# A hybrid decoder layer on one core: the first feed-forward product in a new order, its activation sums on another engine

## The chip, the core and the metric

The kernel runs on one core of a Trainium2 chip. A core has five engines, each with its own queue of instructions that it works off in order: TensorE (PE in the profile; matmuls into PSUM, with PEld for its weight loads), VectorE (DVE), ScalarE (ACT), GpSimd (POOL) and SyncE (SP), which here issues the DMAs. They meet through semaphores. SBUF holds the working tiles, PSUM eight banks of 128 x 512 float32 into which matmuls accumulate. The metric is the time of one execution on the device in microseconds.

## The reference

One decoder layer over 2048 tokens of width 1024, in float32:

```python
h = x + mixed @ w_out                       # mixed: gated linear attention and dilated window attention
nm = rmsnorm(h, mlp_norm_g)
a = jnp.square(jax.nn.relu(nm @ w_ff1))     # 2048 x 1024 times 1024 x 4096
h = h + a @ w_ff2                           # 2048 x 4096 times 4096 x 1024
y = rmsnorm(h, final_norm_g)
```

The change lies in the third line, and in loads for the fourth.

## The kernel before

The stages follow one another: input projection, attention, output projection, first feed-forward product, second feed-forward product. Each float32 operand of a matmul is split into a rounded high part (ScalarE, line 485) and the rest (VectorE, line 486, `split`), and three matmuls (lines 141 to 143, `mm3`) stand for one.

**First product.** The tokens are cut in two halves; the 4096 columns of w_ff1 in 16 groups of 256 (`NP`). A group of one half is a 2 x 2 block product in Strassen's manner, with seven products instead of eight: `jobs1` lists 2 x 16 groups of seven, 224 in all. Each product has four chunks of depth and so 12 matmuls of 128 x 128 by 128 x 512. For one half, the seven combinations of token blocks are kept in SBUF (`TB`, tiles hb), split; `norm_to_T` has written them to DRAM (`hTD`), and `reload` brings one back and splits it in two pieces of 1024 columns. During the last group of the first half, and a little beyond it, the seven of the second half are reloaded product by product (`parts_at`, lines 1570 to 1583).

`prep1(at + 2)` runs ahead of `product1(at)`. It splits the combination of w_ff1 for a product into one of four buffers (`combs1`), and makes the next combinations in place in the raw weights (w1raw, two buffers of 1 MB) with four adds of 512 columns on VectorE. Once the last product of a group has been split, `load_w1(g + 2)` loads the weights of the group after the next into the buffer that has come free. The scheduler may move an instruction ahead of others on its queue by times that it has planned. So the first add of a group (line 1300), which needs only its weights, stands in VectorE's queue almost a group ahead.

`product1` takes one of eight PSUM banks in rotation (`bank`, tags a, c, d, o) for each product. Its results are combined in SBUF: with P1 to P7 the products and X a scratch tile, in the order 1, 2, 5, 6, 3, 4, 7: X = P1; c11 = P2 + X; c22 = P5; X = P6 + X; c12 = X + c22; c12 = P3 + c12; c21 = P4; X = P7 + X; c21 = c21 + X; c22 = c22 + X. Copies run on ScalarE, the seven adds on VectorE. ScalarE then makes relu and square of each of the four blocks, in place. An even group writes them to one of two tiles (`even`), an odd group to one tile (`odd`).

**Sums for the second product.** The second product is a block product of its own with 26 products (`PRODUCTS`), whose left factors are sums of blocks of the activations. After each pair of groups `act_sums` makes them: 28 additions (`SUMS`) of 128 x 256, five after the even group (`EARLY`) and 23 after the odd one, all on GpSimd (line 1333). 22 of them are factors; they go through a ring of eight slots, and each pair is stored to DRAM (`actD`) by SyncE (line 1335). Four more factors are blocks as they are (`single`, line 1362). In all 16 x 28 = 448 additions.

**Second product.** 26 passes of four steps of 24 matmuls. A step's right factor is a combination of w_ff2 (`update_b`: a load, and additions on GpSimd or VectorE, line 1490), split by `prep_b`; its left factor is loaded from `actD` (`load_a`) and split by `prep_a`. The first two steps are prepared within the last products of the first stage (lines 1584 to 1595). At a pass's second step `begin` allocates the outputs whose first use is that pass and loads h into them (line 1536, two loads of 512 KB for each of eight tiles: one tile in pass 0, two in each of passes 1 to 3, one in pass 4). `taken` adds a pass's banks to its outputs during the next pass (line 1543).

SyncE's queue holds all these loads and stores. One that waits, for a sum or a buffer, holds up those behind it. `tc.keep_in_program_order` keeps a DMA from being moved ahead of what the program has before it.

Of the kernel before, what the change touches and what calls it, by code (L numbers as in the profile page):

```python
# [13 lines left out]
AF = mybir.ActivationFunctionType  # L14
# [55 lines left out]
EARLY = 5  # L70
# [45 lines left out]
def emit(tc, a, stop=99):  # L116
# [248 lines left out]
    def bank():  # L365
        banks[0] += 1
        return ps("acao"[banks[0] % 4])
# [906 lines left out]

    w1 = a["w_ff1"].rearrange("o (c p) n -> p (o c) n", p=128)
    NP = FF // 256
    jobs1 = [(g, j) for g in range(2 * NP) for j in order]
    raw1, combs1, acc1 = [], [], []

# [7 lines left out]
    def prep1(at):  # L1287

        if at >= len(jobs1):
            return  # L1290
        g, j = jobs1[at]
        if not combs1:
            combs1.extend(view(c[:, 1024 * q:], (2, 4, 128)) for c in [slot("w1comb", FR) for _ in range(2)]
                          for q in range(2))
        r = raw1[g % 2]
        (a11, a12), (a21, a22) = [[r[:, 4 * k:4 * k + 4, n * 128:n * 128 + 128] for k in range(2)] for n in range(2)]
        c = combs1[at % 4]
        split(c[:, 0], c[:, 1], {1: a11, 2: a12, 5: a21, 6: a21, 3: a12, 4: a22, 7: a21}[j])
        if j == 2:
            V.tensor_tensor(a21, a21, a22, op=OP.add)  # L1300
        if j == 5:
            V.tensor_tensor(a21, a21, a11, op=OP.subtract)  # L1302
            V.tensor_tensor(a12, a12, a21, op=OP.subtract)
        if j == 6:
            V.tensor_tensor(a21, a22, a21, op=OP.subtract)
        if j == 7:
            load_w1(g + 2)

    tags = list("acdcadco")
# [2 lines left out]
        tags.append(tags.pop(0))  # L1312
        return ps(tags[-1])

    xs1, ring1, even, odd = [], [], [], []

    def act_block(name, cs):

# [4 lines left out]
    def act_sums(half, q, cs, which):  # L1323

        if not ring1:
            ring1.extend([view(slot("ring1"), (8, 256)), view(xs1[0][:, 1024:], (4, 256))])
        outs_, temps = ring1
        for name, _, x, op, y in which:
            at = MADE.index(int(name)) if name[0] != "t" else None
            value = lambda v: (act_block(v, cs) if v[0] == "a" else temps[:, int(v[1])] if v[0] == "t"  # L1330
                               else outs_[:, MADE.index(int(v)) % 8])
            dst = temps[:, int(name[1])] if at is None else outs_[:, at % 8]
            G.tensor_tensor(dst, value(x), value(y), op=OP.add if op == "+" else OP.subtract)  # L1333
            if at is not None and at % 2:
                SP.dma_start(actD[at - 1:at + 1, :, q, half].rearrange("r p s -> p r s"), outs_[:, at % 8 - 1:at % 8 + 1])

    def product1(at):
        g, j = jobs1[at]
# [8 lines left out]
        X = xs1[0][:, 512 * par:512 * par + 512]  # L1347
        c11, c12, c21, c22 = [C4[:, n] for n in range(4)]
        both = (even[q % len(even)], C4)
        p = bank()  # L1350
        B, W = TB[j], combs1[at % 4]
        for c in range(4):
            mm3(p, W[:, 0, c], W[:, 1, c], B[0][:, c], B[1][:, c], c == 0, c == 3)

        def square(v):
            A.activation(v, v, AF.Relu)  # L1356
# [4 lines left out]
                if int(name[2]) % 2 == par and 2 * (int(name[2]) // 2) + int(name[1]) // 2 == n:  # L1361
                    SP.dma_start(actD[AT[r], :, q, half], act_block(name, both))

        if j in (1, 5, 4):
            A.activation({1: X, 5: c22, 4: c21}[j], p, AF.Copy)  # L1365
        elif j == 2:
            V.tensor_tensor(c11, p, X, op=OP.add)
            square(c11)
            single(0)
        elif j == 6:  # L1370
            V.tensor_tensor(X, p, X, op=OP.add)
            V.tensor_tensor(c12, X, c22, op=OP.add)
        elif j == 3:
            V.tensor_tensor(c12, p, c12, op=OP.add)  # L1374
            square(c12)
            single(1)
        else:
            V.tensor_tensor(X, p, X, op=OP.add)
            V.tensor_tensor(c21, c21, X, op=OP.add)
            V.tensor_tensor(c22, c22, X, op=OP.add)  # L1380
            square(c21)
            single(2)
            square(c22)
            single(3)
            act_sums(half, q, both, SUMS[EARLY:] if par else SUMS[:EARLY])

    tiles = [8 * half + i + 4 * k for half in range(2) for i in range(4) for k in range(2)]
    nxt = mix_T(tiles[0])
# [137 lines left out]
    def begin(ph):  # L1526

        if "g" not in fin and ph >= 2:
            v = slot("gf")
            fin["g"], fin["scr"] = v[:, :D], v[:, D:2 * D]  # L1530
            SP.dma_start(fin["g"], bcast_row(a["final_norm_g"], D))
        for (k, m), n in began.items():
            if n == ph:
                acc2[k, m] = view(slot("sum"), (4, 512))
                for h in range(2):
                    SP.dma_start(acc2[k, m][:, 2 * h:2 * h + 2],
                                 h6[k // 2, k % 2, :, h, :, 512 * m:512 * m + 512])

    def taken(ph, i, p):

# [33 lines left out]
    for at in range(7, len(jobs1)):  # L1574
        if at == first - 2:
            halves.update({n: reload(order[n], 1) for n in range(2)})
        prep1(at + 2)
        product1(at)
        for n in parts_at.get(at, ()):
            next(halves[n])  # L1580
# [98 lines left out]
```

## Time and profile before

| | |
|---|---|
| median of 3 runs | 2327.23 us (2323.65 to 2327.23) |
| the profiled execution | 2321.99 us, span 2320.2 us |
| mean granted TensorE clock | 0.993 |
| first feed-forward product, first to last matmul start | 1073.0 to 1718 us of the span |
| VectorE idle until the weights landed, before line 1300 | 97.7 us, 30 times |
| SyncE waiting at line 1335 for GpSimd's sums, 1080 to 1700 us | 383.7 us, 159 times |
| TensorE waiting for the low parts of w_ff1, 1080 to 1700 us | 17.2 us, 16 times |

A row of a timeline gives the start in us from the span's start, the duration, the engine, the line, the operation with output and inputs, and in square brackets the idle time of the engine before it and what ended it. A row of busy time by stretch gives the busy us and the number of instructions of each engine, the granted clock, and the share and rate of the DMA engines. An instruction's duration on VectorE overlaps the next one's by some 0.08 us, so queues are counted by the distance of starts.

### The profile page before, as it was taken

How to read it: one execution, taken by the hardware profiler on the slowest of the kernel's cores; microseconds unless marked ns; L12 is line 12 of the kernel's file. 1: busy time of each engine (PE TensorE's matmuls, PEld its weight loads, DVE VectorE, ACT ScalarE, POOL GpSimd, SP SyncE). 2: the span in 40 equal slices, each digit the busy share in tenths (PEclk: the TensorE clock that was granted, in tenths of full speed). 3: DMA queues.
4: the chain of work that ended last, by engine and by line, in shares of the span. 5: the costliest groups of instructions: out<-in, count | busy, mean ns of one | idle time of the engine just before them, and what ended most of it. 6: DMA issues, size and time to landing. Idle time of an engine off the chain costs nothing.

```text
span 2320.2 us, 35443 instructions
## 1 busy us (share of the span) xinstructions
PE 2255.3 (97%) x12508; PEld 1942.2 (84%) x12508; DVE 1646.2 (71%) x2777; ACT 1200.6 (52%) x2404; POOL 954.4 (41%) x914
## 2 busy tenths in 40 slices
PE   9999999999999999999999999999997999999998
PEld 8978998899999988888888877778875888888876
DVE  7787868757767684356766678666675877566788
ACT  6665536427877772235545465454552333333446
POOL 1210002025467571000666757766656553032475
PEclk9999999999999999999999999999998999999999
DMA  5468745777678774588444454454498687577774
GB/s 199 131 192 243 253 133 158 211 232 231 211 212 257 231 236 152 183 277 261 134 147 137 145 180 153 150 170 148 139 317 290 231 276 263 184 247 258 253 255 173
DMA packets 359921, 478.60 MB, mean 206 GB/s; under 512 B 19333, under 2 KB 268694, under 8 KB 347712
## 3 DMA queue, kind: packets, MB, share of 16 engines
q1 hardware_dynamic: 359598, 476.08, 63.5%
q8 instruction: 98, 1.61, 0.3%
q14 instruction: 79, 0.65, 0.1%
q10 hardware_dynamic: 146, 0.27, 0.0%
HBM read 326.54 MB, written 154.44 MB: 207 GB/s over the span
## 4 chain that ended last, share of the span: by engine, by line
PE 64%; DVE 11%; DMA 10%; POOL 5%; ACT 5%; issue 4%; SPq 0%; DVEq 0%; ACTq 0%; POOLq 0%
PE ps_a L142 8%; PE ps_a L143 8%; PE ps_a L141 8%; DMA w1raw<-w_ff 6%; PE ps_c L142 5%; PE ps_c L143 5%; PE ps_c L141 4%; PE ps_a L892 4%; PE ps_o L143 3%; PE ps_o L142 3%; PE ps_o L141 2%; PE ps_d L873 2%; POOL ring L1333 2%; DVE w1comb L486 2%; PE ps_c L851 2%
## 5 line engine op out<-in xcount | busy, mean ns | idle before, releaser
L1490 POOL TENSOR_TENSOR bs<-bs,rb 128x1024 f32<-128x1024 f32 x72 | 215.1, 2995 | 290.8 <-DMA bs<-w_ff 230.7
L485 ACT ACTIVATE cb<-bs 128x1024 fp32r<-128x1024 f32 x104 | 110.1, 1059 | 316.0 <-issue 118.0
L486 DVE TENSOR_TENSOR cb<-bs,cb 128x1024 fp32r<-128x1024 f32 x104 | 176.7, 1700 | 130.7 <-ACT cb L485 129.9
L486 DVE TENSOR_TENSOR w1comb<-w1raw,w1comb 128x512 fp32r<-128x512 f32 x224 | 178.8, 802 | 72.9 <-ACT w1comb L485 72.7
L485 ACT ACTIVATE w1comb<-w1raw 128x512 fp32r<-128x512 f32 x224 | 135.6, 624 | 158.1 <-DVE w1raw L1302 118.2
L1333 POOL TENSOR_TENSOR ring<-acc 128x256 f32<-128x256 f32 x80 | 74.0, 934 | 285.4 <-ACT acc L1357 261.6
L864 ACT ACTIVATE pe<-pe,O 128x256 f32<-128x256 f32 (+1 forms) x384 | 156.5, 453 | 47.0 <-DVE O L863 43.6
L892 PE MATMUL ps_a<-v,pt 128*128 128x65 f32 x1200 | 177.0, 251 | 2.7 <-ACT pt L880 1.9
L892 PEld LDWEIGHTS ps_a<-v,pt 128*128 128x128 f32 x1200 | 173.3, 193 | 4.5 <-ACT pt L880 2.1
L350 POOL TENSOR_TENSOR acc<-acc,misc 128x264 f32<-128x264 f32 (+1 forms) x32 | 38.7, 1220 | 313.1 <-DMA wraw<-w_in 200.3
L873 PE MATMUL ps_d<-ident,pe 128*128 128x128 f32 x600 | 158.6, 277 | 0.0
L863 DVE CUSTOM_DVE_ANT_0 pe<-ps_c,nb 128x256 f32<-128x256 f32 (+1 forms) x384 | 126.2, 360 | 38.3 <-PE ps_d L873 17.1
L1356 ACT ACTIVATE acc<-acc 128x512 f32<-128x512 f32 x128 | 80.1, 631 | 131.1 <-DVE acc L1374 71.6
L285 ACT ACTIVATE wcomb<-wraw 128x512 fp32r<-128x512 f32 (+2 forms) x119 | 90.0, 757 | 98.2 <-PE ps_a L142 35.0
L142 PE MATMUL ps_c<-hb,w1comb 128*128 128x512 f32 x336 | 132.8, 395 | 8.0 <-DVE w1comb L486 7.8
L141 PE MATMUL ps_c<-hb,w1comb 128*128 128x512 f32 x336 | 131.6, 392 | 1.3 <-ACT w1comb L485 1.3
L143 PE MATMUL ps_c<-hb,w1comb 128*128 128x512 f32 x336 | 131.8, 392 | 0.0
L486 DVE TENSOR_TENSOR ca<-ra,ca 128x1024 fp32r<-128x1024 f32 x84 | 119.9, 1431 | 6.1 <-ACT ca L485 6.1
L141 PE MATMUL ps_c<-cb,ca 128*128 128x512 f32 x312 | 122.4, 392 | 0.9 <-ACT acc L1365 0.7
L142 PE MATMUL ps_c<-cb,ca 128*128 128x512 f32 x312 | 122.4, 392 | 0.0
L143 PE MATMUL ps_c<-cb,ca 128*128 128x512 f32 x312 | 122.2, 392 | 0.0
L805 POOL CAST qp<-qs 128x512 fp32r<-128x512 f32 x64 | 68.9, 1161 | 121.3 <-DMA gkD<-acc 104.0
(407 smaller groups left out, 7562.7 us busy)
## 6 DMA issues: line engine op xcount, KB each, us to landing
ra<-actD SPq DMA_DIRECT2D x52, 1024.0 KB, 7.3
actD<-ring SPq DMA_DIRECT2D x176, 256.0 KB, 2.4
rb<-w_ff SPq DMA_DIRECT2D x88, 512.0 KB, 5.0
bs<-w_ff SPq DMA_DIRECT2D x72, 512.0 KB, 6.4
w1raw<-w_ff SPq DMA_DIRECT2D x32, 1024.0 KB, 5.9
k<-kD SPq DMA_DIRECT2D x16, 1024.0 KB, 7.1
rb<-hTD SPq DMA_DIRECT2D x13, 1024.0 KB, 5.9
wraw<-w_in SPq DMA_DIRECT2D x48, 256.0 KB, 3.4
```

The lines of the kernel that those rows point to most:

```text
L141: T.matmul(out, sh, mh, start=first, stop=False, **kw)
L142: T.matmul(out, sl, mh, start=False, stop=False, **kw)
L143: T.matmul(out, sh, ml, start=False, stop=last, **kw)
L285: A.activation(hi, src, AF.Copy, scale=sc)
L485: A.activation(hi, src, AF.Copy)
L486: V.tensor_tensor(lo, src, hi.bitcast(F32), op=OP.subtract)
L863: V.tensor_tensor_reduce(p, s, bias, scale=1.0, scalar=BIG, op0=OP.add, op1=OP.min, accum_out=nm)
L864: A.activation(p, p, AF.Exp, bias=nm, scale=-1.0)
L873: T.transpose(pb[:, i * 128:i * 128 + 128], src, ident)
L892: T.matmul(self.b.opsum[:, n % 4], self.pt[:, i * 128:i * 128 + 128], self.b.v[:, blk, cols], start=first, stop=last)
L1333: G.tensor_tensor(dst, value(x), value(y), op=OP.add if op == "+" else OP.subtract)
L1490: engines[e].tensor_tensor(v, v, r, op=OP.add if op == "+" else OP.subtract)
```

## The change

The order of the seven products becomes 1, 2, 6, 5, 7, 3, 4. Products 6, 7 and 4 go into the PSUM bank of product 1 and accumulate there, and 3 into that of product 5, so that PSUM makes sums that VectorE made: X = P1; c11 = P2 + X; X = P1 + P6; c22 = P5; c22 = (P1 + P6 + P7) + c22; c12 = (P5 + P3) + X; c21 = relu of the whole first bank, read from PSUM. A later product of a bank waits until the bank's last reading is done. The combinations of w_ff1 are made in an order that fits, and the raw buffer is reloaded after product 4. The token blocks are reloaded in the new order.

`act_sums` becomes a generator that yields after each addition; the additions run on VectorE, and `some_sums` issues three of them ahead of each product, and what is left after the last one.

The loads of h in `begin` are kept in program order.

```diff
+    order = (1, 2, 6, 5, 7, 3, 4)
     jobs1 = [(g, j) for g in range(2 * NP) for j in order]
...
-        split(c[:, 0], c[:, 1], {1: a11, 2: a12, 5: a21, 6: a21, 3: a12, 4: a22, 7: a21}[j])
+        split(c[:, 0], c[:, 1], {1: a11, 2: a12, 6: a11, 5: a21, 7: a11, 3: a12, 4: a22}[j])
+        if j == 1:
+            V.tensor_tensor(a21, a21, a22, op=OP.add)
+            V.tensor_tensor(a11, a21, a11, op=OP.subtract)
         if j == 2:
-            V.tensor_tensor(a21, a21, a22, op=OP.add)
-        if j == 5:
-            V.tensor_tensor(a21, a21, a11, op=OP.subtract)
-            V.tensor_tensor(a12, a12, a21, op=OP.subtract)
+            V.tensor_tensor(a12, a12, a11, op=OP.subtract)
         if j == 6:
-            V.tensor_tensor(a21, a22, a21, op=OP.subtract)
-        if j == 7:
+            V.tensor_tensor(a11, a22, a11, op=OP.subtract)
+        if j == 4:
             load_w1(g + 2)
...
-            G.tensor_tensor(dst, value(x), value(y), op=OP.add if op == "+" else OP.subtract)
+            V.tensor_tensor(dst, value(x), value(y), op=OP.add if op == "+" else OP.subtract)
...
+            yield
...
-        p = bank()
+        if j in (1, 2, 5):
+            banks[j] = bank()
+        p = banks[{6: 1, 7: 1, 4: 1, 3: 5}.get(j, j)]
...
-            mm3(p, W[:, 0, c], W[:, 1, c], B[0][:, c], B[1][:, c], c == 0, c == 3)
+            mm3(p, W[:, 0, c], W[:, 1, c], B[0][:, c], B[1][:, c], c == 0 and j in (1, 2, 5), c == 3,
+                skip_group_check=True)
...
-        if j in (1, 5, 4):
-            A.activation({1: X, 5: c22, 4: c21}[j], p, AF.Copy)
+        if j in (1, 6, 5):
+            A.activation(c22 if j == 5 else X, p, AF.Copy)
...
-        elif j == 6:
-            V.tensor_tensor(X, p, X, op=OP.add)
-            V.tensor_tensor(c12, X, c22, op=OP.add)
+        elif j == 7:
+            V.tensor_tensor(c22, p, c22, op=OP.add)
+            square(c22)
+            single(3)
         elif j == 3:
-            V.tensor_tensor(c12, p, c12, op=OP.add)
+            V.tensor_tensor(c12, p, X, op=OP.add)
...
-            V.tensor_tensor(X, p, X, op=OP.add)
-            V.tensor_tensor(c21, c21, X, op=OP.add)
-            V.tensor_tensor(c22, c22, X, op=OP.add)
-            square(c21)
+            A.activation(c21, p, AF.Relu)
+            A.activation(c21, c21, AF.Square)
             single(2)
-            square(c22)
-            single(3)
-            act_sums(half, q, both, SUMS[EARLY:] if par else SUMS[:EARLY])
+            sums1.append(act_sums(half, q, both, SUMS[EARLY:] if par else SUMS[:EARLY]))
+
+    def some_sums(n=3):
+
+        for _ in range(n):
+            while sums1 and next(sums1[0], 0) == 0:
+                sums1.pop(0)
...
-                    SP.dma_start(acc2[k, m][:, 2 * h:2 * h + 2],
-                                 h6[k // 2, k % 2, :, h, :, 512 * m:512 * m + 512])
+                    tc.keep_in_program_order(SP.dma_start(
+                        acc2[k, m][:, 2 * h:2 * h + 2], h6[k // 2, k % 2, :, h, :, 512 * m:512 * m + 512]))
...
         prep1(at + 2)
+        some_sums()
         product1(at)
...
+    some_sums(99)
     held2 = [None, None]
```

More of the change, by code (lines that the diff above doesn't have):

```diff
@@ L1313, in bank @@
         return ps(tags[-1])
-    xs1, ring1, even, odd = [], [], [], []
+    xs1, ring1, even, odd, sums1, banks = [], [], [], [], [], {}
     def act_block(name, cs):
@@ L1577, in emit @@
         prep1(at + 2)
+        some_sums()
         product1(at)
```

## The prediction

> **What bounds the kernel now.** I read the page's first lines, then busy time by stage, then the timelines of VectorE, SyncE and TensorE in the first feed-forward product and at its two seams.
>
> ```profile
> span 2320.2 us, 35443 instructions
> PE 2255.3 (97%) x12508; PEld 1942.2 (84%) x12508; DVE 1646.2 (71%) x2777; ACT 1200.6 (52%) x2404; POOL 954.4 (41%) x914
> ```
>
> TensorE bounds the whole: 97% busy. So the change, which leaves the number of matmuls alone, can only give back time in which TensorE does less than it could. Stage by stage (each engine: busy us and instructions):
>
> ```profile
> core 0: us, PE busy (x) PEld busy (x) DVE busy (x) ACT busy (x) POOL busy (x), PEclk, DMA share, GB/s
> 1073.00:1200.00 127.00, 126.64 (x563) 104.43 (x562) 95.11 (x128) 73.30 (x128) 66.91 (x70) 1.00 0.54 170
> 1200.00:1360.00 160.00, 156.58 (x687) 128.33 (x687) 107.63 (x146) 82.56 (x149) 106.93 (x116) 1.00 0.45 141
> 1360.00:1420.00 60.00, 51.30 (x207) 40.08 (x206) 54.71 (x57) 36.45 (x56) 41.36 (x38) 0.94 0.67 219
> 1420.00:1680.00 260.00, 254.72 (x1116) 208.62 (x1115) 177.70 (x242) 132.87 (x239) 167.40 (x182) 1.00 0.46 146
> 1680.00:1718.00 38.00, 32.83 (x140) 25.59 (x139) 27.63 (x32) 20.09 (x33) 21.02 (x22) 1.00 0.82 270
> 1718.00:1800.00 82.00, 65.84 (x273) 52.72 (x272) 50.99 (x43) 25.86 (x28) 50.26 (x32) 0.92 0.86 307
> 1800.00:2200.00 400.00, 399.91 (x1763) 330.31 (x1762) 284.25 (x251) 149.45 (x155) 140.30 (x48) 1.00 0.72 246
> ```
>
> The last row is undisturbed: 400/1763 = 0.227 us a matmul. A product of 12 is then 2.72 us, a group of seven 19.07. What each stretch did below its length/0.227: 1200 to 1360, 18 matmuls or 4.1 us; 1360 to 1420 (the seam of the halves), 57 or 13.0; 1420 to 1680, 29 or 6.7; 1680 to 1718 (the last group), 27 or 6.2; 1718 to 1800 (start of the second product), 88 or 20.0. Together 50 us: no gain goes beyond it.
>
> Why the steady stretches lose, on VectorE, SyncE and TensorE:
>
> ```profile
> 1211.06 0.69 DVE L1300 TENSOR_TENSOR w1raw<-w1raw 128x512 f32<-128x512 f32 x1 [4.75 <-DMA w1raw<-w_ff]
> ...
> 1212.99 0.68 DVE L1378 TENSOR_TENSOR xs<-ps_a,xs 128x512 f32<-128x512 f32 x1
> ...
> 1223.06 0.69 DVE L486 TENSOR_TENSOR w1comb<-w1raw,w1comb 128x512 fp32r<-128x512 f32 x1 [1.77 <-ACT w1comb L485]
> 1223.67 0.68 DVE L1371 TENSOR_TENSOR xs<-ps_a,xs 128x512 f32<-128x512 f32 x1
> ...
> 1229.29 1.20 DVE L1300 TENSOR_TENSOR w1raw<-w1raw 128x512 f32<-128x512 f32 x1 [2.34 <-DMA w1raw<-w_ff]
> ...
> 1250.79 0.69 DVE L1300 TENSOR_TENSOR w1raw<-w1raw 128x512 f32<-128x512 f32 x1 [4.65 <-DMA w1raw<-w_ff]
> ```
> ```profile
> 1223.78 0.37 SPq L1285 DMA_DIRECT2D w1raw<-w_ff  x1
> ...
> 1244.22 0.42 SPq L1285 DMA_DIRECT2D w1raw<-w_ff  x1
> ```
> ```profile
> 1207.98 0.39 PE L143 MATMUL ps_a<-hb,w1comb 128*128 128x512 f32 x1
> ...
> 1220.13 0.39 PE L143 MATMUL ps_a<-hb,w1comb 128*128 128x512 f32 x1
> ```
>
> This is a ring. VectorE stands still at L1300 until the weights land (1211.06); 12.0 us of its queue later it makes the low part for product 7 (1223.06), the last reader of that buffer; the next load goes out at 1223.78 and ends the next L1300's wait at 1229.29; 14.9 us to the issue at 1244.22, 6.6 more to 1250.79. Two turns take 39.7 us, two groups of matmuls 38.1: the ring, not TensorE, sets the pace. The same rows show how late VectorE runs: the product that ended at 1208.37 in ps_a is taken out at 1212.99, 4.62 us later, and the one that ended at 1220.52 at 1223.67, 3.15 later. With a new bank for every product that costs nothing.
>
> **The change part by part, steady groups.** Matmuls stay 2688. ScalarE keeps 18 instructions a group (7 splits, 3 copies, 8 for the squares; product 4's Relu now reads PSUM): nothing. VectorE loses four of seven 512-wide adds and gains 14 sums of 256 a group (448 over 32). Prices:
>
> ```profile
> 1375.95 1.21 DVE L486 TENSOR_TENSOR hb<-rb,hb 128x1024 fp32r<-128x1024 f32 x1
> 1377.08 1.22 DVE L486 TENSOR_TENSOR w1comb<-w1raw,w1comb 128x512 fp32r<-128x512 f32 x1
> ```
> ```profile
> L863 DVE CUSTOM_DVE_ANT_0 pe<-ps_c,nb 128x256 f32<-128x256 f32 (+1 forms) x384 | 126.2, 360 | 38.3 <-PE ps_d L873 17.1
> ```
> ```profile
> L486 DVE TENSOR_TENSOR w1comb<-w1raw,w1comb x224: 672/685/1226, 1043.2 to 1714.2; 128x512 fp32r<-128x512 f32 x112
> DMA to landing us min/median/max: 5.5/5.9/8.7
> ```
>
> Back to back, 512 columns take 0.61 us (1223.06 to 1223.67), 1024 take 1.13 (1375.95 to 1377.08). No 256-wide add on VectorE is shown: half of the 512 step, 0.31, is the least, 0.36 (the nearest 256-wide row) the most; I take 0.34, on the line through the two steps. A group is then 14 x 0.61 + 14 x 0.34 = 13.3 us; before it was 18 x 0.61 = 11.0 plus what GpSimd takes (the same instruction takes 685 ns at the median and 1226 at most, and 1.22 in the row at 1377.08, while GpSimd works). 107.63 busy us in 1200 to 1360 are 12.8 a group, so VectorE's load hardly changes and its slow instructions go.
>
> The ring shortens. The new order leaves a product between the making of a combination and its split, so of the 12.0 us there remain about five products' work, 5 x 1.90 = 9.5, plus at most the 1.77 wait for ScalarE. SyncE's issue adds 0.4 to 2.3 (it holds stores that now wait for VectorE), the landing 5.5 to 6.6 as in the two turns: 15.4 to 20.2, middle 17, below 19.07. TensorE then sets the pace. Of the 10.8 us in the two steady stretches I take 8 back (0 to 10.8).
>
> Chained products: 6 and 7 follow ScalarE's copies in the bank of 1, 3 its copy in the bank of 5, 4 VectorE's add of 7. One product, 2.72 us, lies between each pair, and a copy or add takes 0.7, so 2 us of lateness are free. On time I cost this at 0; at today's 3.15 to 4.62 us it costs much (first rival). Queued behind a late add are the next splits, which TensorE needs two products on.
>
> The Trainium skill's "Perfetto Trace Analysis", section Matmuls, speaks against this order: independent matmul groups should rotate through different PSUM banks, so that taking one out overlaps the next. By that rule the sum would be the first rival's; the trace shows the lateness that the rotation now hides, but none of it yet in a chained bank.
>
> **The seam of the halves.**
>
> ```profile
> 1374.00:1424.00 50.00, 41.59 (x163) 32.39 (x164) 48.07 (x48) 31.82 (x50) 34.05 (x28) 0.93 0.64 212
> ```
>
> VectorE is full: 48 instructions, 14 of them 1024-wide splits of the reloaded half, worth 14 x 1.13 + 34 x 0.61 = 36.6 us undisturbed, take 48. TensorE gets 163 matmuls in, 13.6 products, 37.0 us of work. After, these need 13.6 x 1.90 + 15.8 = 41.6 on VectorE: 4.6 over, of which the two to three products that are prepared ahead cover some. I leave a loss of 5 of 13.0 and take 8 (3 to 12).
>
> **The last group and the start of the second product.**
>
> ```profile
> 1725.42 9.77 SPq L1536 DMA_DIRECT2D sum<-hD  x7
> ...
> L1536 SPq DMA_DIRECT2D sum<-hD x16: 359/697/1135, 1714.8 to 1738.7; - x16
> DMA to landing us min/median/max: 7.3/10.9/12.6
> ```
> ```profile
> 1746.35 0.74 POOL L1333 TENSOR_TENSOR ring<-xs,ring 128x256 f32<-128x256 f32 x1 [12.54 <-DMA actD<-ring]
> ...
> 1757.70 5.65 POOL L1490 TENSOR_TENSOR bs<-bs,rb 128x1024 f32<-128x1024 f32 x2
> ```
> ```profile
> 1761.18 0.79 PE L141 MATMUL ps_a<-cb,ca 128*128 128x512 f32 x1 [11.85 <-ACT cb L485]
> 1761.78 0.63 PE L141 MATMUL ps_c<-cb,ca 128*128 128x512 f32 x1
> 1762.20 0.63 PE L141 MATMUL ps_d<-cb,ca 128*128 128x512 f32 x1
> ```
> ```profile
> DMA to landing us min/median/max: 2.1/2.4/10.3
> ```
>
> All 16 residual loads (8 MB) go out within 24 us. The stores of the sums queue behind them, GpSimd waits 12.54 us for one, and only at 1757.70 reaches the weight update that ScalarE and TensorE wait for. TensorE loses 11.85 us and then runs slowly (0.42 us a matmul, granted clock 0.92 over the stretch). In program order the loads spread over the first five passes; each is needed 16 us after its issue (three steps of 24 matmuls), against 12.6 at most to land, so that is hidden with 4 to spare. They then stand in SyncE's queue between weight loads that lead by more. GpSimd is free for the weight update. Late next is VectorE: the last 23 sums (7.8 us) and the splits of step 2 (2.3) are 10.1 against 48 matmuls (10.9 us) prepared ahead. The sums now wait on the stores of their ring of eight (four pairs, some 3.4 us apart): nothing at the 2.4 us landing (the last row above, of those stores), some 7 a lap, two laps, at 10.3. So 20.0 shrinks by 4 to 18; I take 12. In the last group VectorE has 14 x 0.61 + 7 x 0.34 + 8 x 1.13 = 20.0 us (the eight are the second product's first updates and splits) for 19.07, without GpSimd's disturbance: 3 of 6.2 (0 to 5).
>
> **Sum.** 8 + 8 + 3 + 12 = 31 (7 to 46). The profiled execution took 2322.0 (span and 1.8 around it): 2291. The median of the runs shown lies 5.2 above it: 2327.2 - 31 = 2296, own range 2281 to 2320.
>
> **The rivals.**
> Evacuation binds: VectorE stays as late as now, and product 4 cannot start in its bank until 7 is taken out. A lateness of 3.15 costs 3.15 + 0.68 - 2.72 = 1.11 us a group, 36 in all; 4.62 costs 2.58, or 83. Less the seams' 23: 2340 to 2387. It turns slower beyond 2.76 us of lateness (23/32 + 2.72 - 0.68). For it: the rows at 1212.99 and 1223.67, and that a wait for weights could be queued ahead of that add. Against: the lateness comes from the ring, which shortens.
> The seams stay: VectorE is as full there as now, or waits on the stores, and only the steady 8 and some 2 come: 2317. For it: 41.6 against 37.0, and landings of 10.3. Against: the residual loads behind those are gone.
> Nothing nets: the sums delay VectorE as much as GpSimd did (13.3 against 12.8 a group) and the seams' gain goes into chained waits: 2327.
>
> **How the numbers follow.** Forecast 0.58, seams stay 0.15, evacuation binds 0.19, nothing nets 0.08. Within 0.2% (4.7 us) a measurement can't tell from no change; so faster 0.73, same 0.08, slower 0.19. The range: down to 2277, all 50 us gained; up to 2338, past "nothing nets" to the near end of the evacuation case, most of which is left out.
>
> **What would show it.** Right: no activity sums on GpSimd; the gap from one load's issue to the next near 19.1 us; 687 matmuls in 156 us; no wait over 5 us at the start of the second product, residual loads over some 85 us (four passes of 96 matmuls); VectorE's 512-wide instructions at 0.69. Wrong: TensorE waiting at L141 for line 1365's copies or for VectorE's add of product 7, in every group; VectorE waiting for the sums' stores; 256-wide sums well over 0.36.

## The result, and the profile after

The changed kernel takes 2289.78 us (median of 4 runs, 2287.84 to 2291.21) against 2325.44 for the kernel before (4 runs beside it, 2322.16 to 2327.23): a ratio of 0.9848, 95% interval 0.9831 to 0.9865. That is 35.7 us less. The profiled execution's span fell by 31.0 us, from 2320.2. The first lines of the page after:

```profile
span 2289.2 us, 35111 instructions
...
PE 2250.7 (98%) x12508; PEld 1946.8 (85%) x12508; DVE 1658.1 (72%) x3097; ACT 1213.8 (53%) x2404; POOL 529.2 (23%) x466
```

GpSimd has lost its 448 sums (914 to 466 instructions), VectorE has 320 more (448 sums, 128 adds fewer). Busy time by stage after, same columns as before, the same stretches of the first product first:

```profile
1200.00:1360.00 160.00, 160.00 (x707) 132.53 (x707) 118.59 (x242) 87.86 (x151) 0.00 (x0) 1.00 0.50 151
1360.00:1420.00 60.00, 55.55 (x237) 45.12 (x236) 51.12 (x85) 41.87 (x66) 0.00 (x0) 0.97 0.63 207
1420.00:1680.00 260.00, 260.00 (x1149) 215.36 (x1148) 193.78 (x388) 144.25 (x247) 0.00 (x0) 1.00 0.52 164
1680.00:1718.00 38.00, 38.00 (x169) 31.46 (x169) 28.66 (x47) 20.13 (x26) 0.00 (x0) 1.00 0.82 283
...
1687.00:1887.00 200.00, 192.23 (x834) 156.65 (x833) 159.65 (x154) 72.11 (x75) 93.81 (x30) 0.99 0.82 287
2167.00:2207.00 40.00, 35.53 (x145) 28.55 (x144) 39.12 (x22) 19.33 (x39) 34.22 (x13) 0.91 0.78 270
```

The last two rows are the first 200 us of the second product and a stretch near its end; the same work lay 31 us later before:

```profile
1718.00:1918.00 200.00, 183.75 (x790) 149.53 (x789) 144.13 (x127) 68.72 (x71) 116.98 (x53) 0.97 0.80 276
2198.00:2238.00 40.00, 36.62 (x154) 29.47 (x153) 40.00 (x23) 20.61 (x43) 33.00 (x12) 0.96 0.77 266
```

At 0.227 us a matmul: the steady stretches now run at TensorE's pace (707 and 1149 matmuls fill 160 and 260 us), so all of the 10.8 us there came back. The seam of the halves loses 60 - 237 x 0.227 = 6.2 in place of 13.0, so 6.8 came back; the last group loses nothing in place of 6.2; the start of the second product gained 834 - 790 = 44 matmuls, 10.0 us. Together 33.8. Near the end 9 matmuls, 2.0 us, were given back. That leaves 31.8 for a span 31.0 shorter.

VectorE's timeline in the same place as before (start, length, line, [idle time before it, and what ended it]), then SyncE's weight loads:

```profile
1205.77 0.68 DVE L1376 TENSOR_TENSOR acc<-ps_d,acc 128x512 f32<-128x512 f32 x1
...
1209.37 0.69 DVE L1301 TENSOR_TENSOR w1raw<-w1raw 128x512 f32<-128x512 f32 x1 [1.60 <-DMA w1raw<-w_ff]
...
1220.20 0.69 DVE L486 TENSOR_TENSOR w1comb<-w1raw,w1comb 128x512 fp32r<-128x512 f32 x1 [1.98 <-ACT w1comb L485]
...
1224.49 0.69 DVE L1376 TENSOR_TENSOR acc<-ps_d,acc 128x512 f32<-128x512 f32 x1 [0.15 <-PE ps_d L143]
...
1226.49 0.69 DVE L1301 TENSOR_TENSOR w1raw<-w1raw 128x512 f32<-128x512 f32 x1 [0.64 <-DMA w1raw<-w_ff]
```
```profile
1202.38 0.37 SPq L1286 DMA_DIRECT2D w1raw<-w_ff  x1
...
1220.92 0.37 SPq L1286 DMA_DIRECT2D w1raw<-w_ff  x1
...
1240.46 0.42 SPq L1286 DMA_DIRECT2D w1raw<-w_ff  x1
```

The ring of weight loads is still there: VectorE still stands still at the hoisted first add until the load lands. But the waits are 1.60 and 0.64 us in place of 4.75 and 2.34, and two turns take 38.08 us (1202.38 to 1240.46), just two groups of matmuls. VectorE is no longer late: at 1224.49 it waits 0.15 for the product that it takes out, where before it came 3.15 to 4.62 us after it; over the 32 groups it waits for product 7 in 14.

At the seam TensorE now stands still twice, for a copy out of a chained bank that the bank's next product has to wait for; below, of ScalarE, the second of these copies and what comes ahead of it:

```profile
1376.31 0.50 PE L141 MATMUL ps_d<-hb,w1comb 128*128 128x512 f32 x1 [2.25 <-ACT xs L1370]
1397.88 0.50 PE L141 MATMUL ps_a<-hb,w1comb 128*128 128x512 f32 x1 [2.20 <-ACT xs L1370]
```
```profile
1394.30 2.01 ACT L485 ACTIVATE hb<-rb 128x1024 fp32r<-128x1024 f32 x2 [2.10 <-DMA rb<-hTD]
...
1397.25 0.58 ACT L1370 ACTIVATE xs<-ps_a 128x512 f32<-128x512 f32 x1
```

The copy at 1397.25 stood behind two splits of the reloaded half, and these behind their load. At the start of the second product the wait of 11.85 us is gone; what is left, and the residual loads:

```profile
1750.86 0.50 PE L142 MATMUL ps_a<-cb,ca 128*128 128x512 f32 x1 [1.96 <-DVE ca L486]
1796.06 0.50 PE L142 MATMUL ps_a<-cb,ca 128*128 128x512 f32 x1 [2.06 <-DVE ca L486]
1837.97 0.50 PE L142 MATMUL ps_a<-cb,ca 128*128 128x512 f32 x1 [3.16 <-DVE ca L1458]
```
```profile
L1544 SPq DMA_DIRECT2D sum<-hD x16: 366/462/1513, 1708.6 to 1801.4; - x16
```

The 16 loads spread over 93 us in place of 24, and no wait is over 3.2 us.

### The profile page after: what moved, and what is told of

Read it like the earlier page. It is cut to its first block, busy times and chain, and to the rows that moved or that the text cites. A ratio compares the mean times of both kernels' runs of the same rounds, so it can differ in the third digit from the quotient of the medians.

```text
span 2289.2 us, 35111 instructions
## 1 busy us (share of the span) xinstructions
PE 2250.7 (98%) x12508; PEld 1946.8 (85%) x12508; DVE 1658.1 (72%) x3097; ACT 1213.8 (53%) x2404; POOL 529.2 (23%) x466
## 4 chain that ended last, share of the span: by engine, by line
PE 83%; DMA 5%; DVE 4%; issue 3%; POOL 3%; ACT 2%; SPq 0%; DVEq 0%; ACTq 0%; POOLq 0%
PE ps_a L142 9%; PE ps_a L141 9%; PE ps_a L143 9%; PE ps_c L141 7%; PE ps_c L142 7%; PE ps_c L143 7%; PE ps_a L892 4%; PE ps_o L143 3%; PE ps_o L142 3%; PE ps_o L141 3%; PE ps_d L142 3%; PE ps_d L141 3%; PE ps_d L143 3%; PE ps_d L873 3%; PE ps_c L851 2%
## 5 line engine op out<-in xcount | busy, mean ns | idle before, releaser
L485 ACT ACTIVATE cb<-bs 128x1024 fp32r<-128x1024 f32 x104 | 110.2, 1060 | 310.7 <-issue 127.2
L486 DVE TENSOR_TENSOR cb<-bs,cb 128x1024 fp32r<-128x1024 f32 x104 | 165.2, 1589 | 112.7 <-ACT cb L485 111.9
L486 DVE TENSOR_TENSOR w1comb<-w1raw,w1comb 128x512 fp32r<-128x512 f32 x224 | 153.7, 688 | 96.3 <-ACT w1comb L485 95.3
L485 ACT ACTIVATE w1comb<-w1raw 128x512 fp32r<-128x512 f32 x224 | 140.2, 627 | 79.3 <-PE ps_c L143 29.5
L141 PE MATMUL ps_c<-hb,w1comb 128*128 128x512 f32 x336 | 130.8, 389 | 0.5 <-ACT xs L1370 0.5
L142 PE MATMUL ps_c<-hb,w1comb 128*128 128x512 f32 x336 | 130.7, 389 | 0.0
L143 PE MATMUL ps_c<-hb,w1comb 128*128 128x512 f32 x336 | 130.1, 389 | 0.0
L486 DVE TENSOR_TENSOR ca<-ra,ca 128x1024 fp32r<-128x1024 f32 x84 | 127.9, 1525 | 0.4 <-ACT ca L485 0.4
L873 PEld LDWEIGHTS ps_d<-ident,pe 128*128 128x128 f32 x600 | 110.5, 188 | 0.1
L141 PE MATMUL ps_a<-wo,mT 128*128 128x512 f32 x256 | 101.3, 396 | 0.0
L1361 ACT ACTIVATE acc<-acc 128x512 f32<-128x512 f32 x96 | 60.7, 632 | 74.8 <-DVE acc L1380 43.3
```

Of the source, the lines that this page charges most:

```text
L141: T.matmul(out, sh, mh, start=first, stop=False, **kw)
L142: T.matmul(out, sl, mh, start=False, stop=False, **kw)
L143: T.matmul(out, sh, ml, start=False, stop=last, **kw)
L485: A.activation(hi, src, AF.Copy)
L486: V.tensor_tensor(lo, src, hi.bitcast(F32), op=OP.subtract)
L873: T.transpose(pb[:, i * 128:i * 128 + 128], src, ident)
```

## The experiments

Twelve kernels. R is the prediction's reason for the steady part: the new order of products shortens the ring of weight loads. G is its rival: what counts is that the sums left GpSimd. Later expectations name further theories, each with its meaning. All ratios are to the kernel before, run beside the kernel on the same chip. "Chained" is the changed kernel's use of PSUM, "own" a bank for each product with seven wide adds on VectorE.

| | order | banks | sums on | residual loads | ratio (95%) | us |
|---|---|---|---|---|---|---|
| after | new | chained | VectorE | in order | 0.9848 (0.9831 to 0.9865) | 2289.78 |
| e1 | new | chained | GpSimd | in order | 0.9852 (0.9837 to 0.9866) | 2290.06 |
| e2 | new | own | VectorE | in order | 0.9822 (0.9807 to 0.9836) | 2282.71 |
| e3 | new | chained | VectorE | free | 0.9848 (0.9831 to 0.9864) | 2289.58 |
| e4 | old | own | GpSimd | in order | 0.9959 (0.9944 to 0.9973) | 2314.58 |
| e5 | new | own | GpSimd | free | 1.0096 (1.0081 to 1.0111) | 2345.68 |
| e6 | new | own | GpSimd | in order | 1.0027 (1.0017 to 1.0038) | 2331.08 |
| e7 | old | own | VectorE | free | 0.9872 (0.9857 to 0.9887) | 2294.21 |
| e9 | old | own | VectorE | in order | 0.9845 (0.9829 to 0.9862) | 2285.71 |

**e1: the sums back on GpSimd.** The changed kernel with this line as before, and each group's sums issued at once after product 4:

```
-            V.tensor_tensor(dst, value(x), value(y), ...)
+            G.tensor_tensor(dst, value(x), value(y), ...)
...
-            sums1.append(act_sums(...))
+            list(act_sums(...))
```

> The changed kernel with the activation sums back on GpSimd, all at once behind each group, as before. Theory R (the ring of weight load, VectorE's queue and next load set the pace, and the new order of combinations shortened it): the steady groups stay at 19.1 us; only the seam and the start of the second product lose, 5 to 15 us, so 2295 to 2305 us. Theory G (GpSimd's sums slowed VectorE, and that set the pace): the steady stretches lose their 11 us again and the start its 10: 2311 us or more, and the stretch 1200 to 1360 holds fewer than 695 matmuls.

The time is that of the changed kernel, and 708 matmuls fill 1200 to 1360. In the changed kernel it doesn't matter where the sums are made. That spoke for R, though R had also expected 5 to 15 us to be lost at the seam and at the start of the second product, and none was.

**e2: a bank for every product again.** The new order stays, X and the corners are summed on VectorE:

```
-        p = banks[{6: 1, 7: 1, 4: 1, 3: 5}.get(j, j)]
+        p = bank()
...
+        elif j == 6:
+            V.tensor_tensor(X, p, X, op=OP.add)
         elif j == 7:
-            V.tensor_tensor(c22, p, c22, op=OP.add)
+            V.tensor_tensor(c12, X, c22, op=OP.add)
+            V.tensor_tensor(X, p, X, op=OP.add)
+            V.tensor_tensor(c22, X, c22, op=OP.add)
...
```

> The changed kernel with a PSUM bank of its own for every product; order, sums on VectorE and loads as changed; the four adds are back on VectorE (15.7 instead of 13.3 us a group). Theory R: VectorE has 3.4 us to spare a group, so the steady groups stay at 19.1 us, and the two waits for ScalarE's copies at the seam of the halves, 2.2 us each, go: 2284 to 2294 us. Theory C (the gain came from taking four adds off VectorE): VectorE falls behind again, 2300 us or more, and TensorE waits for low parts in the steady groups.

7 us faster than e1 and e3, which ran beside it (2281.99 to 2284.2 against 2287.79 to 2293.9). It is the fastest of all kernels here, 1.3 us below R's range, and its steady groups stay full (707 matmuls in 1200 to 1360). Four more adds a group on VectorE cost less than the chaining. The Trainium skill, "Perfetto Trace Analysis", section Matmuls, has independent groups of matmuls rotate through PSUM banks; this run agrees with it, by 7 us.

**e3: the residual loads left to the scheduler**, in the changed kernel:

```
-                    tc.keep_in_program_order(SP.dma_start(...))
+                    SP.dma_start(...)
```

> The changed kernel with the residual loads left to the scheduler, as before. If their crowding of the DMA engines was a cause of its own at the start of the second product: the loads go out within 30 us again, the stores of the sums land late, and VectorE, which now waits for them, holds TensorE up: 2294 to 2304 us. If the stall of before came from GpSimd's backlog alone: 2287 to 2293 us.

No difference. TensorE then waits 5.47 us once for ScalarE's split of ca and 2.09 us for VectorE's, and less often later.

**e4: the loads in program order alone**, in the kernel before:

```
-                    SP.dma_start(...)
+                    tc.keep_in_program_order(SP.dma_start(...))
```

> The kernel before with the residual loads in program order and nothing else. If the loads were a cause of their own: the 11.85 us wait shrinks below 6 us, 2313 to 2320 us. If GpSimd's backlog holds the weight update anyway: 2322 to 2328 us. The steady groups stay as before (687 matmuls in 1200 to 1360) by every theory.

10 us of the 35 come from this line when it stands alone (TensorE's longest wait after 1700 us is 2.9 us, and 685 matmuls in 1200 to 1360 are as before), and none of them in e3, when it is taken out of the whole.

**e5: the new order alone.** The kernel before with the new order of products and combinations, a bank for each, the sums on GpSimd at once, the loads free:

```
+    order = (1, 2, 6, 5, 7, 3, 4)
...
-        split(c[:, 0], c[:, 1], {1: a11, 2: a12, 5: a21, 6: a21, 3: a12, 4: a22, 7: a21}[j])
+        split(c[:, 0], c[:, 1], {1: a11, 2: a12, 6: a11, 5: a21, 7: a11, 3: a12, 4: a22}[j])
...
```

> The kernel before with the new order of products and of the combinations of w_ff1 alone: a bank for every product, seven adds on VectorE, sums on GpSimd at once, residual loads left to the scheduler. Theory R (the new order shortens the ring of load, VectorE's queue and next load): the first product loses its 28 us or so of lateness, the start of the second keeps its stall: 2291 to 2302 us. Rival (the order helps only together with fewer adds on VectorE or without GpSimd on its port): 2308 us or more.

R falls: the new order alone makes the kernel 22 us slower. The stretch 1200 to 1360, VectorE and SyncE in it:

```profile
1200.00:1360.00 160.00, 152.49 (x664) 123.79 (x663) 106.27 (x141) 78.22 (x134) 96.89 (x111) 1.00 0.43 137
```
```profile
1202.87 1.22 DVE L486 TENSOR_TENSOR w1comb<-w1raw,w1comb 128x512 fp32r<-128x512 f32 x1
...
1211.45 0.69 DVE L1301 TENSOR_TENSOR w1raw<-w1raw 128x512 f32<-128x512 f32 x1 [5.62 <-DMA w1raw<-w_ff]
...
1213.20 1.22 DVE L1377 TENSOR_TENSOR acc<-xs,acc 128x512 f32<-128x512 f32 x1
...
1215.48 0.68 DVE L1381 TENSOR_TENSOR acc<-ps_o,acc 128x512 f32<-128x512 f32 x1
```
```profile
1203.57 1.50 SPq L1336 DMA_DIRECT2D actD<-ring  x2
1205.16 0.42 SPq L1286 DMA_DIRECT2D w1raw<-w_ff  x1
```

664 matmuls, fewer than the 687 of the kernel before, and VectorE waits 5.62 for the weights though it is busy only 106 of 160 us. Two things stretch the ring: instructions with both inputs in SBUF take 1.2 us while GpSimd adds, and a load stands 1.07 us behind stores of sums.

**e6: own banks and GpSimd's sums**, with the loads in order: e2 with the edit of e1.

```
-            V.tensor_tensor(dst, value(x), value(y), ...)
+            G.tensor_tensor(dst, value(x), value(y), ...)
```

> A bank for every product, sums on GpSimd at once, residual loads in program order, new order. Against the run with own banks and sums on VectorE (2282.7 us) this moves the sums alone. If it does not matter which engine makes them once the order is new: 2279 to 2287 us. If GpSimd's port costs something where VectorE has 18 wide instructions a group: 2288 us or more.

48 us above e2, for sums that GpSimd makes, all at once behind each group. With chaining the same edit cost nothing (e1).

**e7: the sums on VectorE alone**, in the kernel before: three behind each product, everything else as it was:

```
-            G.tensor_tensor(dst, value(x), value(y), ...)
+            V.tensor_tensor(dst, value(x), value(y), ...)
...
-            act_sums(...)
+            sums1.append(act_sums(...))
...
+        some_sums()
         product1(at)
```

> The kernel before with the sums on VectorE, three ahead of each product, and nothing else. Theory R: the old ring is as long as before or longer (contention falls by some 1.6 us, but five products' sums, 3.4 us, come into it), so the steady stretches keep their loss (680 to 692 matmuls in 1200 to 1360); only the start of the second product gains, at most its 12: 2312 to 2326 us. Theory G (GpSimd on VectorE's port was what slowed the groups): 700 matmuls or more in that stretch, 2305 us or less.

G holds: 2294.21, and the steady part is full without the new order:

```profile
1200.00:1360.00 160.00, 160.00 (x708) 132.60 (x707) 134.95 (x271) 85.22 (x148) 0.00 (x0) 1.00 0.48 151
```

VectorE is far fuller than before (134.95 against 107.63) and TensorE loses nothing. So it was never VectorE's load as such.

**The ring taken apart.** From the timelines of VectorE and SyncE, two turns each, from the issue of the weight load nearest 1200 to the issue of the next but one. "Landing" is the distance from an issue to the row of the hoisted first add, "VectorE" that from this row to the next issue. In it are counted the instructions of 512 columns (0.605 each, back to back) and of 256 (0.335), VectorE's waits, and SyncE's delay after the last low part; "rest" is what these leave.

| | two turns | landings | VectorE | 512 | 256 | waits | SyncE | rest |
|---|---|---|---|---|---|---|---|---|
| before | 39.83 | 12.2 | 27.65 | 29 | 0 | 5.3 | 1.10 | 3.7 |
| e5 | 40.62 | 11.9 | 28.75 | 31 | 0 | 4.5 | 1.10 | 4.4 |
| e7 | 38.08 | 12.3 | 25.78 | 27 | 20 | 1.9 | 0.05 | 0.8 |
| e1 | 38.05 | 12.0 | 26.08 | 20 | 0 | 10.2 | 0.06 | 3.7 |
| after | 38.08 | 12.6 | 25.52 | 19 | 22 | 5.5 | 0.06 | 1.1 |
| e2 | 38.17 | 11.8 | 26.33 | 25 | 25 | 2.0 | 0.06 | 0.7 |

38.1 is two groups of matmuls. In the two kernels whose ring takes more, TensorE has to wait for low parts. The rest is 3.7 to 4.4 us with the sums on GpSimd and about 1 without. The new order puts two more wide instructions into the ring, not fewer (29 to 31). Before needed 1.75 us less. In e7 the rest falls by 2.9 without GpSimd, SyncE's delay by 1.05 and two wide instructions by 1.2; the 20 sums add 6.7, but 3.4 us of VectorE's waits go, and with landings 0.1 longer the sum comes to 1.75. In e1 nine wide instructions fewer give 5.4 and SyncE 1.0; waits that are 4.9 us longer show the slack. Either is enough, and both together give no more.

**e8: more reads of a chained bank.** The changed kernel with three reads more of product 7's bank ahead of the add that product 4 waits for; what they write is overwritten:

```
         elif j == 7:
+            for _ in range(3):
+                V.tensor_tensor(c12, p, c22, op=OP.add)
             V.tensor_tensor(c22, p, c22, op=OP.add)
```

> The changed kernel with VectorE reading product 7's bank three more times before the add that counts (three adds of 512 columns into a tile that is overwritten later), so that the bank comes free 1.8 us later and VectorE does 1.8 us more a group (15.1 of 19.07). If a chained product has 2 us to spare and no more: the add now ends about 0.5 + 2.5 = 3.0 us behind its product against 2.72, TensorE waits at product 4 in most groups, some 0.4 to 0.9 us each: 2300 to 2320 us. If the chain has no such limit: 2289 to 2293 us.

2300.53 (0.99, 0.9884 to 0.9917), 10.8 us above the changed kernel (12 by the ratios). The time lies in the range of the expectation's first case, but its mechanism is not what the trace shows. Some of TensorE's waits from 1060 to 1720 us (us in all, times, the longest):

```profile
PE ps_a L142 <- DVE w1comb L486: 3.8, 7, 0.8
...
PE ps_a L141 <- DVE acc L1378: 1.8, 1, 1.8
...
PE ps_d L141 <- DVE acc L1378: 0.6, 1, 0.6
```

Product 4 waits for the add of product 7 (line 1378) twice in 32 groups, 2.4 us. The low parts of w_ff1, over all banks, take 7.1 us in 15 waits; in 1200 to 1360 one comes every 39 us, as in the kernel before, and two turns of the ring take 39.29 us. The chain has more free than the expectation took, since the scheduler puts other products between 7 and 4. In the changed kernel these are 3 and the next group's 1: 3 follows 7 at 1224.29 and 4 starts at 1229.51, 5.2 us later and not 2.72. In e8 there can be four: 3 follows 7 at 1206.69, the last read of 7 ends at 1214.88, and 4 starts at 1217.57. In places 7 now also runs ahead of 5, and VectorE waits for ScalarE's copy of 5 (22.1 us, 12 times). So the three reads cost through the longer ring, as far as the waits show; the step from the reads to the ring is not shown by a run of its own.

**e9: the two small parts without order and chaining**, e7 with the edit of e4:

```
-                    SP.dma_start(...)
+                    tc.keep_in_program_order(SP.dma_start(...))
```

> The kernel before with two parts of the change alone: the sums on VectorE three behind each product, and the residual loads in program order. The old order of products and a bank for each stay, so VectorE keeps its seven wide adds a group. Theory B (VectorE's burden sets the pace; the sums off GpSimd relieve it, and the new order does nothing more): 2294.2 with the sums alone, less the 8.6 us wait at the start of the second product that the loads in order take away: 2281 to 2288, within 3 us of own banks in the new order (2282.7); 707 or 708 matmuls in 1200 to 1360. Theory R, what is left of it (the new order shortens the ring of weight loads and is worth something of its own): 2290 or more, with fewer than 700 matmuls there or more lost at the seam than in the run with own banks (297 matmuls in 1360 to 1430).

0.9845 against 0.9848: sums on VectorE and loads in order, two small edits, make all of the change's gain. The new order and the chaining together add nothing that these intervals can show. The time and the 707 matmuls in 1200 to 1360 are B's, though not for B's reason, since VectorE is fuller than before (134.99 against 107.63). One sign of R came too: 277 matmuls at the seam (1360 to 1430), where e2 has 297. Whether the new order with own banks (e2, 0.9822) is better than the old one (0.9845) is not settled: the intervals overlap, and the two ran on different chips.

**e10: own banks in the two groups at the seam**, chaining in the other 30, and the adds to match:

```
+        own = g in (NP - 1, NP)
-        if j in (1, 2, 5):
+        if own or j in (1, 2, 5):
             banks[j] = bank()
-        p = banks[{6: 1, 7: 1, 4: 1, 3: 5}.get(j, j)]
+        p = banks[j if own else {6: 1, 7: 1, 4: 1, 3: 5}.get(j, j)]
```

> The changed kernel, with an own bank for every product (and the four extra adds on VectorE) in the two groups on either side of the seam of the halves alone, groups 15 and 16 of 32. Theory C (chaining is paid where ScalarE's copy into X stands behind splits of the reloaded half that wait for their load: the two waits of 2.25 and 2.20 us; elsewhere the chain is covered): the seam gets some 16 matmuls more in 1360 to 1430 (281 to 297), 3.6 us: 2284 to 2287. Rival F (chaining costs a little in every group, or VectorE at the seam becomes the bound with four more adds a group): 2288 to 2292, TensorE waiting at the seam for VectorE's adds or low parts.

0.9854 (0.9837 to 0.9871), no gain on 0.9848. 2286.68 lies within what C expected, but the kernel before was 3 us faster on that chip too, and the trace decides against C. TensorE's three longest waits at the seam, and eight us of it:

```profile
1390.53 0.50 PE L141 MATMUL ps_c<-hb,w1comb 128*128 128x512 f32 x1 [0.92 <-ACT w1comb L485]
1393.04 0.50 PE L141 MATMUL ps_d<-hb,w1comb 128*128 128x512 f32 x1 [1.49 <-ACT hb L485]
1395.51 0.80 PE L141 MATMUL ps_c<-hb,w1comb 128*128 128x512 f32 x1 [1.96 <-ACT w1comb L485]
```
```profile
1392.00:1400.00 8.00, 4.99 (x12) 3.71 (x13) 8.00 (x16) 3.46 (x6) 0.00 (x0) 0.64 0.57 167
```

The two chained waits went, and three waits for ScalarE's splits came, with a slower clock behind them: 269 matmuls in 1360 to 1430 in place of 281. F's sign, TensorE waiting there for VectorE, did not come either. e9, with own banks in the old order, has the same three waits (0.30, 1.49 and 2.48 us). ScalarE waits for the reloads in e10 (6.5 us, four times) and in e2 (5.5, four times) alike, so this does not tell the two apart.

**e11: e8's three reads with own banks** (e2 with the edit of e8).

> Own banks in the new order (2282.7), with three reads more of product 7's bank by VectorE ahead of its add, 1.8 us, as in the run that cost the changed kernel 11 us; what they write is overwritten by the adds that follow. VectorE then has 16.1 + 1.8 = 17.9 us of work in 19.07 a group, more than in that run (15.9). Theory C (that run's price was product 4 waiting in its chained bank): it costs less here though VectorE is fuller, 2283 to 2288, and 1200 to 1360 keeps 700 or more matmuls. Theory L (it was VectorE's load): 2293 or more.

2291.68 (0.9876, 0.9858 to 0.9895), some 12 us above e2 by the ratios: more than C expected, less than L, and as much as e8 lost. Where it is lost differs; the stretches 1200 to 1360, 1360 to 1430 (the seam) and 1430 to 1680 of e8, then of e11:

```profile
1200.00:1360.00 160.00, 157.39 (x687) 127.93 (x686) 127.06 (x260) 80.64 (x148) 0.00 (x0) 1.00 0.47 144
1360.00:1430.00 70.00, 62.70 (x260) 48.95 (x259) 61.80 (x108) 43.95 (x70) 0.00 (x0) 0.98 0.61 203
1430.00:1680.00 250.00, 246.73 (x1077) 201.04 (x1075) 196.81 (x394) 126.41 (x231) 0.00 (x0) 1.00 0.47 146
```
```profile
1200.00:1360.00 160.00, 160.00 (x708) 132.51 (x707) 146.56 (x295) 77.08 (x139) 0.00 (x0) 1.00 0.48 147
1360.00:1430.00 70.00, 63.79 (x264) 50.91 (x263) 64.99 (x111) 42.62 (x68) 0.00 (x0) 0.95 0.56 188
1430.00:1680.00 250.00, 249.31 (x1101) 206.17 (x1100) 236.00 (x475) 125.73 (x222) 0.00 (x0) 1.00 0.50 161
```

With own banks the steady stretches stay full though VectorE is busy 146.56 of 160; chained, they lose 20 and 27 matmuls (against 707 and 1104), 10.7 us, at 127.06. So it is with chaining that the three reads cost something in the steady groups, but not by the wait that C names (e8). At the seam e11 does 33 matmuls fewer than e2's 297, 7.5 us; TensorE waits there 3.7 us once for ScalarE's split and 2.1 for low parts, with VectorE busy 64.99 of 70, so L is possible there and not shown.

**e12: additions on GpSimd that no store and no sum follows**, in e2; they write into X, which no one reads again until product 1's copy two groups on:

```
+            for n in range(14):
+                x, y = (c21[:, :256], c22[:, :256]) if n == 0 else (X[:, :256], X[:, 256 if n > 1 else 0:][:, :256])
+                G.tensor_tensor(X[:, 256 * (n > 0):][:, :256], x, y, op=OP.add)
             sums1.append(act_sums(...))
```

> Own banks in the new order with the sums on VectorE (2282.7), and beside them 14 additions of 128 x 256 a group on GpSimd that nothing waits for and that are not stored: they write into X of the group's parity, which no one reads again before product 1's copy two groups later. SyncE's queue is as it was. Theory P (what the sums on GpSimd cost is that VectorE's instructions run longer beside them): two turns of the ring of weight loads take 6.2 + 5.6 to land and 11.0 + 15.4 on VectorE, 36.1 without the 2.0 in which VectorE waits; the sums on GpSimd lengthened VectorE's two stretches by 3.2 (before) to 4.3 (new order alone), so 39.3 to 40.4 against 38.1: 665 to 690 matmuls in 1200 to 1360, some 512-wide instructions at 1.2 us, 2293 to 2312. Theory Q (it is SyncE: stores that wait for GpSimd hold up the weight loads, 1.07 us every second load): 705 or more matmuls, 2281 to 2287.

2424.27 (1.0437, 1.0419 to 1.0455), 4% slower than before. P's mechanism shows in the trace, Q's times are far off, and P's size was far too small. Two turns of the ring take 46.40 us, and 579 matmuls are done in 1200 to 1360. GpSimd, then VectorE beside it:

```profile
1213.45 11.70 POOL L1390 TENSOR_TENSOR xs<-xs 128x256 f32<-128x256 f32 x13
```
```profile
1216.95 0.94 DVE L1334 TENSOR_TENSOR ring<-xs,ring 128x256 f32<-128x256 f32 x1
1217.81 0.94 DVE L1334 TENSOR_TENSOR ring<-acc,xs 128x256 f32<-128x256 f32 x1
1218.67 1.21 DVE L486 TENSOR_TENSOR w1comb<-w1raw,w1comb 128x512 fp32r<-128x512 f32 x1
...
1223.29 0.68 DVE L1371 TENSOR_TENSOR acc<-ps_c,xs 128x512 f32<-128x512 f32 x1
```

VectorE's own sums, which the estimate had not counted as slowed, go from 0.335 to 0.86 us apart. The stretch from 1205.26 to the next load holds the same 14 wide and 20 narrow instructions as in e2 and takes 22.74 us in place of 15.36. But not all of the loss is P's. The additions were not free of followers: ScalarE's copy of product 1 into X waited for the last of them 8 times, 41.6 us in all, 4.2 of it in 1200 to 1360 and 29.8 in 1430 to 1680. So the run shows that the contention is real and lengthens the ring, in 1200 to 1360 above all; its 2424.27 is not the price of contention alone.

## Why the prediction came out right, and where its reasons did not

The forecast was 2296 (range 2277 to 2338), with 31 us to gain in the profiled execution; the runs gave 2289.78, and the spans differ by 31.0. The terms: steady groups 8, measured 10.8; seam 8, measured 6.8; last group 3, measured 6.2; start of the second product 12, measured 10.0; and 2.0 given back near the end, which no term had. That the total meets 31.0 so closely is luck: the terms are off by 1.2 to 3.2 us each, and most of the errors cancel.

**The bound.** TensorE bounds the whole and the gain lies in the four places named: right. All 10.8 us of the steady part came, as its upper bound had it.

**The ring.** That it set the pace was right: in the four kernels of the table whose two turns take about 38.1 us TensorE is full, in the two where they take more it is not. The step that failed is "The new order leaves a product between the making of a combination and its split, so of the 12.0 us there remain about five products' work". It counted one of the two turns, the short one (12.7 and 14.9 us on VectorE), and gave to the order what came from elsewhere. So the steady term came out for a reason that it did not have, and that is luck too. The order alone lengthens the ring to 40.62 (e5). What shortens it in the changed kernel is the ten wide instructions fewer that chaining in this order leaves there (29 to 19), and GpSimd's silence; either would have done (e1, e7). The size, 15.4 to 20.2 a turn, still held: 19.0, or 16.3 without VectorE's waits.

**Prices.** A sum of 256 columns takes 0.335 us back to back (predicted 0.34), and the low parts run undisturbed, as predicted:

```profile
L486 DVE TENSOR_TENSOR w1comb<-w1raw,w1comb x224: 680/691/695, 1044.9 to 1687.6; 128x512 fp32r<-128x512 f32 x112
```

**Chained products.** Costed at nothing when on time. In the steady groups that is what they cost: VectorE waits for the product, not the other way about. "One product, 2.72 us, lies between each pair" was too little for 7 and 4, with 5.2 us between them in the trace. At the seam the cost of nothing was wrong, since the prediction left out what stands ahead of ScalarE's copies: a chained product waits for a copy behind the splits of the reloads, 2.25 and 2.20 us. Taking the chaining out there only moves the wait (e10); taking it out everywhere is worth 7 us (e2). Why e2 keeps its waits at the seam under 0.8 us and e10 and e9 don't is open.

**The start.** The wait of 11.85 went, as predicted, with both causes named, GpSimd's backlog and the residual loads. The loads weigh more: in e4 no wait over 2.9 us is left though GpSimd still makes the sums, while in e7, with the sums moved and the loads free, one of 8.6 us stays (5.47 in e3). The gains don't add: the loads in order give 10 alone (e4), some 6 with the sums already moved (e7 to e9, 0.9872 to 0.9845, their intervals just overlapping), none in the whole (e3). What is late next is VectorE, as the prediction had it.

**The rivals.** Evacuation binds: by its sum it needed 2.76 us of lateness, and now VectorE waits for product 7 (1224.49). With 5.2 us between 7 and 4 it would have needed some 2.5 more (an estimate from these two numbers), and e8, meant to bring it about, has product 4 waiting in two groups only; that e8 costs 10.8 us all the same shows how little room the kernel has, but not this rival. The seams stay: the seam kept 6.2 of its 13.0, not all. Nothing nets: it did not come. Half the change nets nothing beside the other half (e9), but not because the sums delay VectorE.

## What to carry to other kernels

When a change has several parts, ask for each what it gives if the others are already there: here ordering the loads cured the stall at the start and moving the sums shortened it, moving the sums and chaining each cured the ring, and two short edits (e9) gave all that the rewriting gave. Count a loop that runs through a queue by every instruction between the load and its next issue, over a whole period, and compare it with the time of the work it feeds; a busy share says little (in 1200 to 1360, with VectorE at 92%, TensorE lost nothing in e11; with VectorE at 67%, it lost 18 of 705 matmuls in the kernel before). Where a run costs what a theory expects, look whether the wait that the theory names is in the trace (e8). An engine beside the path can set the pace by slowing another through what they share.

## What the runs showed of the hardware

Beside additions on GpSimd, VectorE's instructions with two inputs in SBUF take about twice as long: 512 columns 1.22 us in place of 0.69, 256 columns 0.94 in place of 0.42. Those with one input in PSUM keep 0.68 (1215.48 in e5, 1223.29 in e12). The Trainium skill, "SBUF — State Buffer", section Who interferes with whom, says just this of the two kinds; the traces agree, and add the sizes.

The granted clock falls after short waits too: 0.64 over 8 us behind waits of 0.92, 1.49 and 1.96 us within six us (e10), where e2, with waits of 0.55, 0.79 and 0.73 at its seam, keeps 1.00:

```profile
1389.73 0.50 PE L141 MATMUL ps_a<-hb,w1comb 128*128 128x512 f32 x1 [0.55 <-ACT w1comb L485]
1391.25 0.50 PE L141 MATMUL ps_o<-hb,w1comb 128*128 128x512 f32 x1 [0.79 <-ACT w1comb L485]
1393.86 0.50 PE L141 MATMUL ps_c<-hb,w1comb 128*128 128x512 f32 x1 [0.73 <-ACT hb L485]
```
```profile
1392.00:1400.00 8.00, 7.27 (x32) 5.67 (x32) 8.00 (x14) 2.64 (x3) 0.00 (x0) 1.00 0.69 199
```

After 1395.51 in e10 the first matmul takes 0.80 us in place of 0.39.
